# Sums of the latents' squares by one-column matmuls, and the last output block in finer pieces, in a two-layer decoder trunk

## The chip, the core and the metric

The kernel runs on one core of one Trainium2 chip. A core has a matrix engine (TensorE, PE in the profile; PEld is its loading of weights), VectorE (DVE), ScalarE (ACT), GpSimd (POOL) and SyncE (SP, which here only starts transfers). Each engine works through its own list of instructions in order; semaphores make one wait for another. The metric is the device time of one execution in microseconds, as the median of several.

## What is computed

Two layers, one sequence of 1024 tokens, width 1024, all in float32. Cut to what matters here:

```python
for l in range(DEPTH):                                  # 2
    h = x * (1.0 + scale[:, None, :]) + shift[:, None, :]
    (p_cq, p_ckv, p_kr, p_qb, ..., p_gate) = jnp.split(h @ w_in[l], SPLIT_POINTS, axis=-1)
    cq = rms_norm(p_cq, q_norm_g[l])                    # 768 columns
    ckv = rms_norm(p_ckv, kv_norm_g[l])                 # 256 columns
    ...                                                 # three groups of attention heads
    sub = y @ w_out[l]
    x = layer_norm(ALPHA * x + (1.0 + gate[:, None, :]) * sub, ln_g[l], ln_b[l])
```

`rms_norm` divides a token's row by the root of the mean of its squares. The change concerns the sums of squares of `cq` and `ckv`, and the last block of the last layer's `layer_norm`.

## The kernel before

Every float32 matrix is split into a high and a low part, and a product is three matmuls (line 206). Activations are held transposed, features on partitions and tokens in columns. A projection (`project`, line 209) makes 128 features for all tokens, in two halves of 512 columns, each a chain of 24 matmuls into one PSUM bank of the pool `ps_p` (tile `pj`, two banks); a function `evac` then empties the bank. Other banks are `ps_s` (tile `S`, three) for scores, `ps_t` (tile `T`, two) for transposes, and `o_ps` (tile `O`).

Each layer runs the indexer (scores of all keys into `acc`, line 441), then heads B, the selection of 256 keys a row (`select`, 31 rounds of counting over `acc` on VectorE, line 467, and ScalarE, line 485), heads C, heads A, and the output projection. The code names these one after another, but a scheduler interleaves them and fixes each engine's order when the kernel is built; it decides by durations that it assumes, so other instructions can give another order everywhere behind them.

Eight calls of `latent` in each layer make `ckv` (two calls, sums in `rk`) and `cq` (six calls, sums in `scq`). Two of them are called right behind the indexer, before heads B; the others are spread between heads B. For each half, `evac` squares the bank into `sq` (line 614), and the sum over the 128 features, which lie on partitions, is made in two steps: four transposes of 128x128 into a bank `T` (line 619), and a reduction on VectorE of the bank's 512 columns to 4 (line 622 for the first chunk of a sum, line 625 for the later ones, with an addition in line 626). `norm_r` (line 644) then takes the power -1/2 on GpSimd.

The same banks `T` serve the attention's transposes of probabilities (line 320), which ScalarE and VectorE empty (lines 323, 324). GpSimd scales probabilities (line 298), computes low parts of weights (line 198) and multiplies by gates (line 339). Lines 229 to 238 empty the projections of queries and keys; a bank `pj` is free once line 238 has read it.

The output projection (line 853 on) goes over eight blocks of 128 tokens, in each over two halves of 512 columns: 24 matmuls, then on VectorE a product (line 868), an addition (869) and statistics (870); when both halves are done, the statistics are merged, and in the last layer two operations for each half (879, 880) and a store started by SyncE (881) end the block.

Of the kernel before, what the change touches and what calls it, by code (L numbers as in the profile page):

```python
# [8 lines left out]
F32 = mybir.dt.float32  # L9
# [3 lines left out]
AF = mybir.ActivationFunctionType  # L13
OP = mybir.AluOpType
AX = mybir.AxisListType
# [5 lines left out]
S = 1024  # L21
P = 128
# [13 lines left out]
TBO = (7,6,5,4,3,2,1,0)  # L36
# [72 lines left out]
def trunk(ctx: ExitStack, tc: tile.TileContext, a, out):  # L109
# [494 lines left out]
    def latent(l, i):  # L604

        wh, wl = w_chunk(l, CKV + i)
        g = gkv[:, i:i + 1] if i < 2 else gq[:, i - 2:i - 1]
        sums = rk if i < 2 else scq

        def evac(half, cols, ps):  # L610
            hi, lo, sq = RW.next().bitcast(F32R), RW.next().bitcast(F32R), PR.next()
            act.activation(hi, ps, AF.Copy, scale=g)
            dve.scalar_tensor_tensor(lo, ps, g, bc(hi), OP.mult, OP.subtract)
            act.activation(sq, ps, AF.Square)
            for e, part in enumerate((hi, lo)):
                sp.dma_start(cq_d[:, (2 * i + e) * 1024 + half * 512:(2 * i + e) * 1024 + half * 512 + 512], bc(part))
            t = ps_t.tile([P, 4, P], F32, name="T")
            for j in range(4):
                pe.transpose(t[:, j, :], sq[:, j * P:(j + 1) * P], ident)
            to = sums[:, half * 4:half * 4 + 4]  # L620
            if i in (0, 2):
                dve.tensor_reduce(to, t, AX.X, OP.add)
            else:
                s4 = small.tile([P, 4], F32, name="s4")
                dve.tensor_reduce(s4, t, AX.X, OP.add)
                dve.tensor_tensor(to, to, s4, OP.add)

        project(wh, wl, 8, HA, evac)
        if i == 1:
            norm_r(rk, rk, 256, 1e-6, 1.0)  # L630
        elif i == 7:
            norm_r(scq, scq, 768, 1e-6, -float(96 ** -0.5))
# [177 lines left out]
    def out_proj(l):  # L810
        last = l == DEPTH - 1
        order = [3, 4, 5, 6, 7, 0, 1, 2]
        Y = HA
        for k in order[:5]:
            raw = WR.next()
            sp.dma_start(raw, y_d[k])
            act.activation(Y[k][0], raw, AF.Copy)
            (pool if k in YP[l] else dve).tensor_tensor(Y[k][1], raw, bc(Y[k][0]), OP.subtract)  # L818


        Vs = [VS[0][:, i * 1024:(i + 1) * 1024] for i in range(6)]
        f = G.n % 2 ^ 1
        XR = Ring([AC[0], RES] + ([G.tiles[f]] if last else []))
        at = {3: (Vs[4], Vs[5]), 4: (Vs[0], Vs[1]), 5: W.tiles[0:2], 6: W.tiles[2:4],
              7: (fresh(f"g{1 - f}", F32R), fresh("bi1", F32R)), 0: held[0:2], 1: held[2:4],
              2: (Vs[2], [fresh(f"rw{n}", F32R, 512) for n in range(2)])}
        wo = {}
        for k in order:
            raw = WR.next()
            sp.dma_start(raw, a["w_out"][l, k])  # L830
            hi, lo = at[k]
            eng = pool if k in WP[l] else dve
            for n in range(2):
                c = slice(n * 512, n * 512 + 512)
                act.activation(hi[:, c], raw[:, c], AF.Copy)  # L835
                eng.tensor_tensor(lo[n] if k == 2 else lo[:, c], raw[:, c], bc(hi[:, c]), OP.subtract)
            wo[k] = [(hi[:, n * 512:n * 512 + 512], lo[n] if k == 2 else lo[:, n * 512:n * 512 + 512]) for n in range(2)]
        g1 = BI.tiles[0]
        sp.dma_start(g1, g1_d[l].to_broadcast([P, 1024]))
        if last:  # L840
            sp.dma_start(LNG, a["ln_g"][l].to_broadcast([P, 1024]))
            sp.dma_start(LNB, a["ln_b"][l].to_broadcast([P, 1024]))
        else:

            lnc = small.tile([P, 2, 8], F32, name="lnc", bufs=1)
            sp.dma_start(lnc, a["ln_c"])
            dve.tensor_tensor(lnc[:, 0, :], lnc[:, 0, :], scale1_n, OP.mult)
            dve.tensor_tensor(lnc[:, 1, :], lnc[:, 1, :], scale1_n, OP.mult)
            dve.tensor_tensor(lnc[:, 1, :], lnc[:, 1, :], shift_n, OP.add)
        X = Ring(AC[1:4] + [PR3[0]])  # L850
        PR.tiles = [G.tiles[f]]
        xs = {}
        for tb in TBO:
            tok = slice(tb * P, (tb + 1) * P)
            xr = XR.next()
            sp.dma_start(xr, xw_d[tb] if last else a["x"][tb])
            r = X.next()
            st = small.tile([P, 2, 6], F32, name="st")
            for n in range(2):
                cols = slice(n * 512, n * 512 + 512)  # L860
                ps = (ps_p if n else ps_s).tile([P, 512], F32, name="pj" if n else "S")
                items = []
                for k in order:
                    yh, yl = Y[k]
                    w0, w1 = wo[k][n]
                    items += [(yh[:, tok], w0), (yl[:, tok], w0), (yh[:, tok], w1)]
                chain(ps, items)
                dve.tensor_tensor(r[:, cols], ps, g1[:, cols], OP.mult)
                dve.scalar_tensor_tensor(r[:, cols], xr[:, cols], ALPHA, r[:, cols], OP.mult, OP.add)
                dve.bn_stats(st[:, n, :], r[:, cols])  # L870
            mv = small.tile([P, 2], F32, name="mv")
            dve.bn_aggr(mv, st)
            rs = small.tile([P, 1], F32, name="rs")
            dve.tensor_scalar(rs, mv[:, 1:2], 1e-5, None, OP.add)
            pool.tensor_tensor(rs, rs, mhalf, OP.pow)
            if last:
                for n in range(2):
                    cols = slice(n * 512, (n + 1) * 512)
                    dve.scalar_tensor_tensor(r[:, cols], r[:, cols], mv[:, 0:1], LNG[:, cols], OP.subtract, OP.mult)
                    dve.scalar_tensor_tensor(r[:, cols], r[:, cols], rs, LNB[:, cols], OP.mult, OP.add)  # L880
                    sp.dma_start(out[tb][:, cols], r[:, cols])
                continue
            dve.tensor_scalar(r, r, mv[:, 0:1], rs, OP.subtract, OP.mult)
            sp.dma_start(x1_d[tb], r)
            xs[tb] = r
            if len(xs) == 4:
                for k in range(8):
                    t = ps_t.tile([P, 512], F32, name="T")
                    for j in range(4):
                        pe.transpose(t[:, j * P:(j + 1) * P], xs[tb // 4 * 4 + j][:, k * P:(k + 1) * P], ident)  # L890
                    mod_h(t, tb // 4, k, PR.next(), lnc[:, 0, :], lnc[:, 1, :])
                xs = {}
# [193 lines left out]
```

## Time and profile before

| what | us |
|---|---|
| three timed runs | 1753.45, 1750.38, 1753.22 |
| their median | 1753.22 |
| the profiled execution, its own time | 1750.43 |
| its span (first to last instruction) | 1748.6 |

The profile records one execution: for each instruction its engine, source line, start, duration and the idle time of its engine just before it, with the instruction or transfer that ended this idle time. A page sums it up; views of the trace group instructions by line, list who waited for whom, show the order of time in a stretch, or give each engine's busy time in windows. "Granted clock" is the share of TensorE's full clock in a window. The slices of the page below have each 1/40 of the span, and a digit is the busy share in tenths:

```profile
PE   8999899999999999989999999999999899998998
DVE  6888898888588678885772668889876967778777
ACT  4254599895534666675112656999744357667620
```

### The profile page before, as it was taken

What the parts mean: (1) busy time and instruction counts of PE and PEld (TensorE: products, weight loads), DVE (VectorE), ACT (ScalarE), POOL (GpSimd) and SP (SyncE); (2) the same over time, 40 slices, a digit from 0 to 9 for tenths busy, and PEclk for the clock granted to TensorE, in tenths of its full rate; (3) what the DMA queues carried; (4) which work ended last, traced back from release to release, by engine and by line L of the source; (5) the groups of instructions that cost most, each with busy time, mean ns of one, the idle gap of its engine ahead of it and who ended that gap; (6) DMA issues with size and microseconds to landing.
All of it is one profiled execution on the core that took longest, in us unless ns stands there. A gap on an engine that the chain in (4) does not pass through costs nothing.

```text
span 1748.6 us, 26930 instructions
## 1 busy us (share of the span) xinstructions
PE 1673.0 (96%) x9192; PEld 1451.5 (83%) x9192; DVE 1350.5 (77%) x3213; ACT 1019.8 (58%) x2010; POOL 666.9 (38%) x614
## 2 busy tenths in 40 slices
PE   8999899999999999989999999999999899998998
PEld 8888688888887888878898977888789788987886
DVE  6888898888588678885772668889876967778777
ACT  4254599895534666675112656999744357667620
POOL 0221143323434355463346413333243344657421
PEclk9999999999999999999999999999999999999999
DMA  9665023233202521222343421333221227113122
GB/s 367 212 215 189 25 73 97 70 136 91 79 35 54 221 90 58 73 70 93 125 157 124 168 73 49 85 111 95 73 97 50 60 52 265 47 52 124 49 86 95
DMA packets 57668, 187.32 MB, mean 107 GB/s; under 512 B 7862, under 2 KB 8886, under 8 KB 57020
## 3 DMA queue, kind: packets, MB, share of 16 engines
q1 hardware_dynamic: 53116, 156.25, 26.3%
q0 software_dynamic: 4416, 29.36, 5.8%
q8 instruction: 72, 1.18, 0.3%
q14 instruction: 64, 0.52, 0.1%
HBM read 133.94 MB, written 39.07 MB: 99 GB/s over the span
## 4 chain that ended last, share of the span: by engine, by line
PE 53%; DVE 8%; ACT 3%; issue 2%; DMA 1%; POOL 1%; DVEq 0%; ACTq 0%; POOLq 0%
PE pj L204 30%; PE S L204 12%; PE O L332 5%; PE T L320 5%; DVE pt L324 1%; ACT pt L323 1%; PE T L204 1%; ACT scr L485 1%; DVE acc L543 0%; DVE pr L536 0%; DVE acc L441 0%; PE T L890 0%; DVE h L818 0%; DVE acc L291 0%; ACT pr L296 0%
## 5 line engine op out<-in xcount | busy, mean ns | idle before, releaser
L204 PE MATMUL pj<-h,w 128*128 128x512 f32 (+1 forms) x3408 | 833.0, 391 | 13.9 <-DVE qk L238 5.8
L204 PEld LDWEIGHTS pj<-h,w 128*128 128x128 f32 x3408 | 629.9, 190 | 131.1 <-issue 11.9
L198 POOL TENSOR_TENSOR w<-wr,w 128x1024 fp32r<-128x1024 f32 (+2 forms) x86 | 192.4, 2238 | 302.3 <-ACT w L197 290.1
L204 PE MATMUL S<-qk,qk 128*128 128x512 f32 (+2 forms) x1104 | 279.7, 358 | 8.4 <-DVE mx L288 3.1
L323 ACT ACTIVATE pt<-T 128x512 fp32r<-128x512 f32 (+1 forms) x320 | 172.4, 551 | 111.2 <-PE T L320 53.8
L298 POOL TENSOR_SCALAR pr<-pr,den 128x896 f32<-128x896 f32 (+7 forms) x180 | 139.0, 776 | 253.3 <-DVE den L297 223.9
L324 DVE TENSOR_TENSOR pt<-T,pt 128x512 fp32r<-128x512 f32 (+1 forms) x320 | 199.5, 633 | 43.9 <-ACT pt L323 37.9
L332 PE MATMUL O<-pt,v 128*128 128x256 f32 (+1 forms) x1280 | 212.8, 286 | 9.2 <-DVE pt L324 4.1
L485 ACT ACTIVATE scr<-acc,U 128x768 uint8<-128x768 f32 x186 | 193.2, 1038 | 35.6 <-DVE U L481 18.1
L204 PEld LDWEIGHTS S<-qk,qk 128*128 128x128 f32 x1104 | 184.2, 190 | 33.4 <-DVE mx L288 6.4
L332 PEld LDWEIGHTS O<-pt,v 128*128 128x128 f32 x1280 | 186.1, 191 | 26.7 <-DVE pt L324 6.7
L339 POOL TENSOR_TENSOR g<-g,osum 64x256 f32<-64x256 f32 x128 | 98.9, 773 | 235.0 <-DVE osum L337 222.8
L296 ACT ACTIVATE pr<-pr,mx 128x384 f32<-128x384 f32 (+7 forms) x188 | 145.5, 775 | 48.1 <-DVE mx L288 31.2
L320 PE MATMUL T<-ident,pr 128*128 128x128 f32 x852 | 145.4, 279 | 6.3 <-POOL pr L298 3.1
L467 DVE TENSOR_SCALAR_CACHE_REDUCE scr<-acc,U 128x384 uint8<-128x384 f32 x186 | 138.2, 743 | 3.8
L197 ACT ACTIVATE w<-wr 128x1024 fp32r<-128x1024 f32 (+2 forms) x86 | 83.8, 976 | 69.2 <-PE pj L204 59.7
L320 PEld LDWEIGHTS T<-ident,pr 128*128 128x128 f32 x852 | 102.1, 142 | 18.7 <-POOL pr L298 4.2
L204 PE MATMUL pj<-w,h 128*128 128x256 f32 (+2 forms) x672 | 107.0, 300 | 0.2 <-ACT w L835 0.2
L204 PEld LDWEIGHTS pj<-w,h 128*128 128x128 f32 x672 | 91.7, 190 | 5.1 <-ACT w L835 0.5
L336 ACT ACTIVATE osum<-O 64x256 f32<-64x256 f32 x128 | 48.6, 380 | 63.4 <-PE O L332 60.3
L441 DVE SCALAR_TENSOR_TENSOR acc<-S,wi,acc 128x512 f32<-128x512 f32 (+1 forms) x84 | 55.7, 678 | 23.0 <-ACT S L436 22.8
L337 DVE TENSOR_TENSOR osum<-O,osum 64x256 f32<-64x256 f32 x128 | 53.5, 418 | 25.1 <-ACT osum L336 21.4
(282 smaller groups left out, 2512.2 us busy)
## 6 DMA issues: line engine op xcount, KB each, us to landing
wr<-in_wt_dram SPq DMA_DIRECT2D x62, 512.0 KB, 3.9
cq_d<-rw SPq DMA_DIRECT2D x64, 256.0 KB, 2.0
h<-cq_d POOLq DMA_DIRECT2D x4, 4096.0 KB, 19.1
qk<-qk POOLq DMA_DIRECT2D x48, 256.0 KB, 3.0
pt<-in_w_ada_dram SPq DMA_DIRECT2D x22, 512.0 KB, 4.7
wr<-in_w_out_dram SPq DMA_DIRECT2D x16, 512.0 KB, 3.5
bi<-in_bias_dram SPq DMA_DIRECT2D x14, 512.0 KB, 3.7
bi<-in_w_ada_dram SPq DMA_DIRECT2D x10, 512.0 KB, 4.4
```

The lines of the kernel that those rows point to most:

```text
L197: act.activation(hi[:, :n], raw[:, :n], AF.Copy)
L198: (lo_eng or pool).tensor_tensor(lo[:, :n], raw[:, :n], bc(hi[:, :n]), OP.subtract)
L204: pe.matmul(ps, lhsT=l, rhs=r, start=(i == 0), stop=(i == len(items) - 1))
L296: act.activation(p[:, :n], p[:, :n], AF.Exp, bias=m, scale=-1.0, accum_out=den)
L298: (dve if ne[qb] else pool).tensor_scalar(p[:, :n], p[:, :n], den, 0.5, OP.mult, OP.mult)
L320: pe.transpose(t[:, c:c + P], p[j](2 * kp + kk), ident)
L323: act.activation(pt[:, 0, :n], t[:, :n], AF.Copy)
L324: dve.tensor_tensor(pt[:, 1, :n], t[:, :n], bc(pt[:, 0, :n]), OP.subtract)
L332: pe.matmul(o[:, oc], lhsT=vt(kb), rhs=pt[:, e, pc], start=(kb == 0 and e == 0), stop=(kb == 2 * g + 1 and e == 1), skip_group_check=True)
L339: pool.tensor_tensor(yc, yc, s[r0:r0 + 64], OP.mult)
L467: dve.tensor_scalar(scr8[:, :IDX_LEN[b]], scores(b), s, None, op, OP.add, accum_out=dst[:, b:b + 1])
L485: act.activation(scr[:, :IDX_LEN[b]], scores(b), AF.Sign, bias=U[:, b:b + 1].bitcast(F32), accum_out=cnt[:, b:b + 1])
```

## The change

The four transposes of a half become four matmuls with the squares as weights and a column of ones as the moving operand: each gives one column with the sums over the 128 features, for 128 tokens. The 4 columns are copied out by ScalarE, and the additions of later chunks go to GpSimd. Separately, the last block of the last layer makes its second half as two chains of 256 columns, takes its statistics over pieces of 256, and starts its second store from ScalarE's queue.

```diff
-            t = ps_t.tile([P, 4, P], F32, name="T")
+            to = sums[:, half * 4:half * 4 + 4]
+
+            t = ps_t.tile([P, 512], F32, name="T")
             for j in range(4):
-                pe.transpose(t[:, j, :], sq[:, j * P:(j + 1) * P], ident)
-            to = sums[:, half * 4:half * 4 + 4]
+                pe.matmul(t[:, j:j + 1], lhsT=sq[:, j * P:(j + 1) * P], rhs=ones, start=True, stop=True,
+                          skip_group_check=True)
             if i in (0, 2):
-                dve.tensor_reduce(to, t, AX.X, OP.add)
+                act.activation(to, t[:, 0:4], AF.Copy)
             else:
                 s4 = small.tile([P, 4], F32, name="s4")
-                dve.tensor_reduce(s4, t, AX.X, OP.add)
-                dve.tensor_tensor(to, to, s4, OP.add)
+                act.activation(s4, t[:, 0:4], AF.Copy)
+                pool.tensor_tensor(to, to, s4, OP.add)
...
-            st = small.tile([P, 2, 6], F32, name="st")
-            for n in range(2):
-                cols = slice(n * 512, n * 512 + 512)
-                ps = (ps_p if n else ps_s).tile([P, 512], F32, name="pj" if n else "S")
+
+            end = last and tb == TBO[-1]
+            st = small.tile([P, 4, 6], F32, name="st4", bufs=1) if end else small.tile([P, 2, 6], F32, name="st")
+            for o, w in ((0, 512), (512, 256), (768, 256)) if end else ((0, 512), (512, 512)):
+                n, cols = o // 512, slice(o, o + w)
+                bank = (ps_p if n else ps_s).tile([P, 512], F32, name="pj" if n else "S")
+                ps, part = bank[:, :w], slice(o % 512, o % 512 + w)
                 items = []
                 for k in order:
                     yh, yl = Y[k]
                     w0, w1 = wo[k][n]
-                    items += [(yh[:, tok], w0), (yl[:, tok], w0), (yh[:, tok], w1)]
+                    items += [(yh[:, tok], w0[:, part]), (yl[:, tok], w0[:, part]), (yh[:, tok], w1[:, part])]
                 chain(ps, items)
...
-                dve.bn_stats(st[:, n, :], r[:, cols])
+                if end:
+                    for i in range(o, o + w, 256):
+                        dve.bn_stats(st[:, i // 256, :], r[:, i:i + 256])
+                else:
+                    dve.bn_stats(st[:, n, :], r[:, cols])
...
-                    cols = slice(n * 512, (n + 1) * 512)
+                    cols, queue = slice(n * 512, n * 512 + 512), act if end and n else sp
...
-                    sp.dma_start(out[tb][:, cols], r[:, cols])
+                    queue.dma_start(out[tb][:, cols], r[:, cols])
```

What this does to the engines' lists is seen at two places. The first is the junction between the indexer and the selection of layer 0 (layer 1 has the same), VectorE's list with - for before and + for now; `T`, `pj` and `S` are banks, `qk` queries and keys, `rk` the sums of `ckv`, `cnt` counts of the selection:

```order
 L441 SCALAR_TENSOR_TENSOR acc<-S,wi,acc 128x512
-L622 TENSOR_REDUCE rk<-T 128x4
 L467 TENSOR_SCALAR scr,cnt_127<-acc 128x512
 L231 TENSOR_TENSOR qk_76<-pj,qk_76 64x512
 L441 SCALAR_TENSOR_TENSOR acc<-S,wi,acc 128x512
 L446 TENSOR_TENSOR acc<-acc,causb 128x128
-L622 TENSOR_REDUCE rk<-T 128x4
 L238 TENSOR_TENSOR qk_78<-pj,qk_77 64x512
 L467 TENSOR_SCALAR scr,cnt_127<-acc 128x640
-L625 TENSOR_REDUCE s_1551<-T 128x4
+L648 TENSOR_SCALAR rk<-rk 128x8
 L238 TENSOR_TENSOR qk_78<-pj,qk_77 64x512
```

Both reductions ahead of the first line 238 are gone, and the first step of `norm_r` (now line 648) has moved up between the two lines 238. At the same place ScalarE's list now reads:

```order
L229 ACTIVATE qk_76<-pj 64x512
L436 ACTIVATE S<-S 128x512
L624 ACTIVATE rk<-T 128x4 x2
L237 ACTIVATE qk_77<-pj 64x512
L627 ACTIVATE s_1551<-T 128x4
L627 ACTIVATE s_1589<-T 128x4
L237 ACTIVATE qk_77<-pj 64x512
L485 ACTIVATE scr,cnt<-acc,U 128x768
```

The four copies stand between the emptyings of the projection, ahead of the selection's first pass (line 485). The second place is GpSimd's list among the heads B of layer 0, now: `pr` are probabilities, `den` their divisors, `w` parts of weights:

```order
+L628 TENSOR_TENSOR scq<-scq,s_2985 128x4
 L298 TENSOR_SCALAR pr_94<-pr_94,den 128x128
+L628 TENSOR_TENSOR scq<-scq,s_3023 128x4
 L298 TENSOR_SCALAR pr_94<-pr_94,den 128x256
 L198 TENSOR_TENSOR w_87<-wr_92,w_86 128x1024
+L628 TENSOR_TENSOR scq<-scq,s_3064 128x4
 L298 TENSOR_SCALAR pr_95<-pr_95,den 128x384
+L628 TENSOR_TENSOR scq<-scq,s_3102 128x4
 L298 TENSOR_SCALAR pr_95<-pr_95,den 128x512
```

The additions stand between the scalings of probabilities. Behind the junction the scheduler has also put the work of heads B, C and A and of the selection in another order, in both layers; the indexer, and the output projection of the first layer up to the next junction, keep theirs on TensorE.

## The prediction

> **What bounds the kernel now.** First the page: what each engine does and what the chain of waits that ended last is made of.
>
> ```profile
> span 1748.6 us, 26930 instructions
> PE 1673.0 (96%) x9192; PEld 1451.5 (83%) x9192; DVE 1350.5 (77%) x3213; ACT 1019.8 (58%) x2010; POOL 666.9 (38%) x614
> PE 53%; DVE 8%; ACT 3%; issue 2%; DMA 1%; POOL 1%; DVEq 0%; ACTq 0%; POOLq 0%
> ```
>
> TensorE is busy for all but 75.6 us of the span and leads the chain; VectorE comes next with 8%. So work taken from VectorE is worth only what TensorE waits for it. The second view is the list of waits, the third the instructions of the lines that the change touches.
>
> ```profile
> PE T L619 <- DVE rk L622: 7.3, 4, 2.2
> L619 PE MATMUL T<-ident,pr x128: 270/273/477, 192.4 to 1294.2; 128*128 128x128 f32 x128
> L626 DVE TENSOR_TENSOR scq<-scq,s x20: 143/162/1652, 323.9 to 1296.7; 128x4 f32<-128x4 f32 x20
> ```
>
> The first row says (total us, times, longest us): TensorE waited 7.3 us in four waits for the reductions of line 622. They are the stage that matters, once in each layer, where the indexer ends and the selection begins. Third view, the order of time there in layer 0 (start, duration, the idle time and its releaser in brackets), then the two rows that matter in layer 1:
>
> ```profile
> 196.60 1.12 PE L619 MATMUL T<-ident,pr 128*128 128x128 f32 x4 [1.64 <-DVE rk L622]
> 199.50 1.12 PE L619 MATMUL T<-ident,pr 128*128 128x128 f32 x4 [1.79 <-DVE rk L622]
> 200.27 0.78 PE L204 MATMUL pj<-h,w 128*128 128x512 f32 x1
> 195.86 0.68 DVE L622 TENSOR_REDUCE rk<-T 128x4 f32<-128x512 f32 x1
> 196.46 0.68 DVE L467 TENSOR_SCALAR_CACHE_REDUCE scr<-acc 128x512 uint8<-128x512 f32 x1
> 198.76 0.68 DVE L622 TENSOR_REDUCE rk<-T 128x4 f32<-128x512 f32 x1
> 199.48 0.69 DVE L238 TENSOR_TENSOR qk<-pj,qk 64x512 fp32r<-64x512 f32 x1
> 1053.89 0.69 DVE L238 TENSOR_TENSOR qk<-pj,qk 64x512 fp32r<-64x512 f32 x1
> 1054.68 0.78 PE L204 MATMUL pj<-h,w 128*128 128x512 f32 x1
> ```
>
> The third and the fourth group of transposes (196.60, 199.50) wait for a bank T that VectorE must first sum. VectorE itself is hardly idle here. After the last group a long run of projections starts, and its bank is freed at 200.17 by line 238, at the same moment.
>
> The same stretch in windows as long as the clock's steps (columns: length, busy us of PE, PEld, DVE, ACT, POOL with counts, the granted clock, DMA):
>
> ```profile
> 192.87:196.28 3.41, 0.89 (x7) 0.42 (x4) 3.35 (x8) 1.49 (x3) 0.00 (x0) 1.00 0.01 2
> 196.28:199.70 3.42, 1.31 (x5) 0.92 (x6) 3.32 (x8) 0.59 (x1) 0.55 (x1) 0.50 0.00 0
> 199.70:203.11 3.41, 3.41 (x11) 2.83 (x11) 3.25 (x7) 0.00 (x0) 0.33 (x1) 0.50 0.37 77
> 1053.03:1056.44 3.41, 2.52 (x8) 2.22 (x9) 3.28 (x8) 0.00 (x0) 0.57 (x1) 0.50 0.37 77
> 1056.44:1059.85 3.41, 3.41 (x9) 2.64 (x9) 3.35 (x8) 0.00 (x0) 0.51 (x1) 0.50 0.37 77
> 49.51:52.92 3.41, 3.34 (x28) 3.25 (x27) 1.97 (x6) 2.30 (x2) 0.08 (x1) 1.00 0.39 137
> 49.51:52.92 3.41, 1.84 (x16) 1.93 (x16) 1.00 0.39 137
> 52.92:56.33 3.41, 3.41 (x12) 3.41 (x11) 1.93 (x4) 2.30 (x2) 0.00 (x0) 0.50 0.88 282
> ```
>
> After a poorly filled window the clock is granted at 0.50 for two windows, and the first projections run at half speed. The last three rows give a warning: the window at 49.51 is full of TensorE work, but 16 of its 28 matmuls, 1.84 us of it, are the one-column matmuls of line 925 (the row with PE and PEld alone), and the next window gets 0.50. One-column matmuls seem not to hold the clock.
>
> **The change, part by part.**
>
> *TensorE.* 128 transposes become 128 one-column matmuls. Their price is the spacing of the weight loads in a closed run:
>
> ```profile
> 313.57 0.75 PEld L619 LDWEIGHTS T<-ident,pr 128*128 128x128 f32 x7
> 139.91 1.75 PEld L266 LDWEIGHTS O<-ones,g 128*128 128x128 f32 x14
> ```
>
> Transposes: (0.75 - 0.14)/6 = 0.10 us, 0.14 being one load. One-column matmuls with the same ones: (1.75 - 0.19)/13 = 0.12 us, at a load of 0.19. Where TensorE is full the change costs 0.02 us each; the 32 at the junctions below stand in idle time, so 96 x 0.02 = 1.9 us is the upper bound, 0 the lower (single groups differ by as much), and I take **+1.0**.
>
> *VectorE* loses 32 reductions x 0.68 + 24 additions x 0.16 = 25.6 us, of which 8 x 0.68 + 4 x 0.15 = 6.0 stand at the two junctions.
>
> *ScalarE and GpSimd* get 32 copies and 24 additions of 128x4, which no row has. Nearest rows:
>
> ```profile
> L250 ACT ACTIVATE cs<-ccol 128x8 f32<-128x8 f32 x1 | 0.2, 209 | 0.3 <-DMA ccol<-in_c_dram 0.3
> L336 ACT ACTIVATE osum<-O 64x256 f32<-64x256 f32 x128 | 48.6, 380 | 63.4 <-PE O L332 60.3 <-POOL pr L298 0.7
> L1076 POOL MEMSET const-float32-1.0<- 128x1 f32 x1 | 0.1, 98 | 0.0
> L339 POOL TENSOR_TENSOR g<-g,osum 64x256 f32<-64x256 f32 x128 | 98.9, 773 | 235.0 <-DVE osum L337 222.8 <-PE pj L204 7.0 <-PE T L320 3.9
> ```
>
> A copy costs 0.21 (near the 8-column row) to 0.38 us; an addition 0.10 to 0.77, and I take 0.2, twice the one-column fill. That is 6.7 and 4.8 us on engines 58% and 38% busy, hidden by their idle time; where the cover fails is the slower rival below.
>
> *The junctions.* ScalarE is almost idle there (1.49 and 0.59 us in the first two windows), so the banks come free early and all four groups are done near 196. TensorE then waits for the projection bank, that is for line 238. Ahead of it VectorE loses both reductions of line 622: 196.46 - 195.86 = 0.60 and 199.48 - 198.76 = 0.72, together 1.32 us. The projections start at 198.95 in place of 200.27; only 1.3 of the 5 us idle are won, since line 238 is late next. The wait that is added, VectorE's line 648 for two additions on GpSimd, has the second line 238 and the selection queued behind it; but the additions can end near 198, and VectorE arrives near 199.7, so it costs nothing unless an addition takes over 0.77.
>
> Those 1.32 us lie at half clock: worth 0.66 if both half-speed windows stay. In layer 1 the window from 1053.03 would now be filled but for 0.3 us, and if that ends the half speed at 1056.44, the work done by 1059.85 is 3.08/2 + 3.41 = 4.95 in place of 5.17/2 = 2.59: worth 2.4. How the windows fall differs between executions, so I take the middle, 1.5 a junction, **-3.1** (bounds -1.3 to -4.8).
>
> *The rest of the selection.* 25.6 - 6.0 = 19.6 us leave VectorE in these stretches:
>
> ```profile
> 210.00:560.00 350.00, 340.41 (x1862) 291.37 (x1861) 287.58 (x769) 248.32 (x484) 127.49 (x119) 1.00 0.26 79
> 1060.00:1300.00 240.00, 236.85 (x1224) 200.49 (x1223) 204.53 (x602) 198.54 (x385) 83.06 (x80) 0.99 0.28 87
> ```
>
> TensorE idles only 9.6 + 3.2 = 12.8 us in them. VectorE loses 4% of its 492 us; 4% of the idle time is **-0.5**, bounds 0 and -12.8. The scheduler also puts the work of both stretches in another order; the rows cannot price that, and it adds a few us either way to the range.
>
> *The last block.* The chain for columns 512 to 1023 becomes two of 256 columns, so that VectorE's last three operations are half as long.
>
> ```profile
> 1734.71 5.45 PE pj L204 x24
> 1358.36 3.12 PE L204 MATMUL pj<-w,h 128*128 128x256 f32 x24
> 1741.64 0.69 DVE L870 BATCH_NORM_STATS2 st<-pr 128x6 f32<-128x512 f32 x1
> L441 DVE SCALAR_TENSOR_TENSOR acc<-S,wi,acc 128x512 f32<-128x512 f32 x27 | 20.0, 748 | 17.5 <-ACT S L436 17.4
> L441 DVE SCALAR_TENSOR_TENSOR acc<-S,wi,acc 128x256 f32<-128x256 f32 x7 | 3.3, 476 | 0.7 <-ACT S L436 0.7
> 1744.00 1.41 DVE L880 SCALAR_TENSOR_TENSOR pr<-pr,rs,lnb 128x512 f32<-128x512 f32 x2
> 1744.78 0.99 SPq L881 DMA_DIRECT2D out_dram<-pr  x2
> ```
>
> TensorE pays: (3.12 - 0.28)/23 = 0.1235 us for each of 48 is 5.93 against 5.45, +0.5. VectorE gains 748 - 476 = 0.27 on each of three operations, -0.8; for the statistics (0.69 at 512) no row at 256 exists, and their part lies between 0 and 0.27. The second store on ScalarE's queue gains nothing: SyncE's two issues end at 1745.77, 0.36 after the data at 1745.41, so the second never stood behind the first. Net **-0.3** (-0.6 to 0).
>
> Sum: +1.0 - 3.1 - 0.5 - 0.3 = **-2.9 us**. The profiled execution took 1750.43 in all (span 1748.6) and would take 1747.5; the three timed runs have the median 1753.22, and would give 1750.3. I forecast the middle, 1751.8 - 2.9 = **1748.9**.
>
> **The rivals.** B, *the half speed goes*. For it: the waits of TensorE get shorter. Against it: the four groups of one column would leave the window at 192.87 as empty for the clock as the one at 49.51. If it went in both layers, the junctions give 1.32 + 2.84/2 = 2.7 and 1.32 + 5.17/2 = 3.9, 6.6 in place of 3.1, and the time is 1748.9 - 3.5 = 1745.4. The Trainium skill (TensorE: Matmul & The Clock Gate, section on what's actually happening) has the clock fall after at least one idle window of some 3.4 us, which by itself would spare a 2.9 us gap like the new one. The trace disagrees: no window above was idle, and 0.89 of 3.41 busy was too little.
>
> C, *the junctions give nothing*: what TensorE wins it loses at its next wait for the same VectorE, and neither they nor the stretches give anything: 1751.8 + 1.0 - 0.3 = 1752.5. For it: 96% busy, so a start 1.3 us earlier may meet the next late operand; against it: VectorE itself runs 3 us ahead after the junction.
>
> D, *slower*: copies stand behind selection passes on ScalarE, additions behind copies on GpSimd, and GpSimd's scaling of line 298 behind additions.
>
> ```profile
> L485 ACT ACTIVATE scr<-acc,U x186: 920/1041/1161, 207.5 to 1255.0; 128x768 uint8<-128x768 f32 x62, 128x896 uint8<-128x896 f32 x62, 128x1024 uint8<-128x1024 f32 x62
> POOL pr L298 <- DVE den L297: 223.9, 113, 9.0
> ```
>
> Line 298 stands directly behind an addition in 9 places, and a copy can wait for one pass, 1.04 us and 0.19 for its accumulator. If all 9 delay TensorE it costs 11.1: 1748.9 + 11.1 = 1760.0; with half of them the time is 1754.5, a loss of 2.7. It decides where an addition ends later than the reciprocal that line 298 has always waited for; those waits (113, 2 us each) speak for slack.
>
> **How the numbers follow.** Forecast 0.50 (own range 1744.5 to 1751), B 0.11, C 0.21, D 0.18. About 0.2%, 3.5 us, can be told from no change. Faster (under 1748.3): 0.35 of the forecast, which a larger gain in the stretches or at the junctions would bring, and B, together 0.46. Same (to 1755.3): the rest of the forecast, 0.16 of C and 0.05 of D, 0.36. Slower: 0.05 of C and 0.13 of D, 0.18. The range takes in B, the larger gains and most of D: 1741 to 1758.
>
> **What would show it.** Right: no wait of TensorE for line 622's successors, projections at 198.9 released by line 238, selection some 3 us earlier, copies near 0.2 us, the last VectorE chain 0.8 shorter after a TensorE chain 0.5 longer. Wrong: clock 1.00 after the junctions (B), waits of line 298 for line 628 or of line 628 for ScalarE (D), or idle time of TensorE that moves by over 5 us in the attention stretches, which would be the new order rather than the operations.

## The result, and the profile after

| | us |
|---|---|
| before, four runs | 1750.38 to 1753.45, median 1752.40 |
| the change, four runs | 1769.47 to 1773.03, median 1770.32 |
| ratio, with its 95% interval | 1.0107 [1.0095, 1.0120] |
| span of the profiled execution | 1769.3 (before 1748.6) |

The change makes the kernel slower by 18 us, past the upper end of the range (1758). The page of the changed kernel has the answer in its second line:

```profile
span 1769.3 us, 27269 instructions
PE 1696.0 (96%) x9344; PEld 1474.3 (83%) x9344; DVE 1329.2 (75%) x3161; ACT 1021.5 (58%) x2042; POOL 672.7 (38%) x638
PE 68%; DVE 17%; ACT 8%; issue 4%; DMA 2%; POOL 1%; SPq 0%; DVEq 0%; ACTq 0%; POOLq 0%
```

TensorE's idle time (span less busy) is 73.3 us against 75.6 before: no engine has begun to hold it up. Its busy time has grown by 23.0 us, and its instructions by 152. Of these the last block has 24. The other 128 stand in the groups of the line of the sums (count, busy us, mean ns of one, idle time before them and what ended it); the first row is the kernel before:

```profile
L619 PE MATMUL T<-ident,pr 128*128 128x128 f32 x128 | 20.7, 291 | 9.7 <-DVE rk L622 7.3 <-DVE acc L441 2.4
L621 PEld LDWEIGHTS T<-ones,pr 128*128 128x128 f32 x256 | 35.0, 213 | 2.7 <-ACT rk L624 1.0 <-DVE acc L441 0.9
L621 PE MATMUL T<-ones,pr 128*128 128x1 f32 x256 | 34.5, 261 | 0.8 <-ACT rk L624 0.8
```

The code asks for 128 one-column matmuls; the record has 256 weight loads and 256 matmuls. A matmul of plain float32 operands is two such pairs here, a transpose of the same 128x128 block was one. (The matmuls of the projections are recorded once each, 24 rows for a chain of 24: the kernel marks their operands as `float32r`, and the views print `f32` for both.) In the order of time, 16 loads for the eight matmuls of two halves take 1.98 us:

```profile
324.56 1.98 PEld L621 LDWEIGHTS T<-ones,pr 128*128 128x128 f32 x16
```

At the junction of layer 0 TensorE's order of time is now:

```profile
194.47 1.05 PE L621 MATMUL T<-ones,pr 128*128 128x1 f32 x8
195.93 4.54 PE L621 MATMUL T<-ones,pr 128*128 128x1 f32 x24 [0.41 <-ACT rk L624]
201.04 5.49 PE L204 MATMUL pj<-h,w 128*128 128x512 f32 x12 [0.58 <-DVE qk L238]
```

The waits for line 622 (7.3 us at both junctions) are gone; 0.41 us is left here, 0.8 at both. In the kernel before, the first group of transposes there began at 192.44 and the projections at 200.27, 7.83 us later; now it is 201.04 - 194.47 = 6.57. In windows of the clock's steps (length, busy us of PE, PEld, DVE, ACT, POOL with counts, granted clock, DMA):

```profile
193.37:196.78 3.41, 3.00 (x20) 2.12 (x18) 3.38 (x9) 2.51 (x7) 0.00 (x0) 1.00 0.01 2
196.78:200.19 3.41, 3.41 (x18) 3.41 (x18) 3.31 (x8) 0.94 (x3) 0.20 (x1) 0.50 0.00 0
200.19:203.61 3.42, 2.84 (x8) 2.28 (x8) 3.30 (x8) 0.77 (x2) 2.19 (x3) 0.50 0.30 61
203.61:207.02 3.41, 3.41 (x9) 2.64 (x9) 3.20 (x11) 0.05 (x1) 0.76 (x2) 0.50 0.47 97
```

The first two windows are 88% and 100% busy, mostly with one-column matmuls, and still three steps are granted at half clock, one more than before. In layer 1 three steps follow too.

Away from the junctions no drop of the clock begins behind the sums. The next two rows (TensorE alone) are a window with 16 one-column matmuls, 1.70 us of it, and its successor; the last two are a window without any, but with gaps, and its successor:

```profile
323.07:326.48 3.41, 3.41 (x25) 1.00 0.38 154
326.48:329.89 3.41, 3.41 (x20) 1.00 0.00 0
282.11:285.53 3.42, 1.73 (x9) 1.00 0.24 84
285.53:288.94 3.41, 3.06 (x15) 0.50 0.24 84
```

Ahead of the last block the trace has 19 steps at half clock, where the kernel before had 14. Six of the 19 stand at the two junctions, where four stood. The drops elsewhere begin behind windows in which line 621 does not run, as at 282.11 (TensorE busy for 1.73 of 3.42 us).

### The profile page after: what moved, and what is told of

Its sections match the earlier page's. It is cut to its first block, busy times and chain, and to the rows that moved or that the text cites. A ratio compares the mean times of both kernels' runs of the same rounds, so it can differ in the third digit from the quotient of the medians.

```text
span 1769.3 us, 27269 instructions
## 1 busy us (share of the span) xinstructions
PE 1696.0 (96%) x9344; PEld 1474.3 (83%) x9344; DVE 1329.2 (75%) x3161; ACT 1021.5 (58%) x2042; POOL 672.7 (38%) x638
## 4 chain that ended last, share of the span: by engine, by line
PE 68%; DVE 17%; ACT 8%; issue 4%; DMA 2%; POOL 1%; SPq 0%; DVEq 0%; ACTq 0%; POOLq 0%
PE pj L204 40%; PE S L204 13%; PE O L332 6%; PE T L320 5%; ACT scr L485 3%; DVE pt L324 2%; ACT pt L323 1%; DVE scr L467 1%; DVE pr L288 1%; DVE pr L536 1%; ACT pr L296 1%; PE T L204 1%; DVE g L261 1%; DVE acc L441 1%; PE S L920 1%
## 5 line engine op out<-in xcount | busy, mean ns | idle before, releaser
L204 PE MATMUL S<-qk,qk 128*128 128x384 f32 (+2 forms) x1104 | 279.0, 359 | 7.5 <-DVE mx L288 4.7
L288 DVE CUSTOM_DVE_ANT_0 pr<-S,bi 128x384 f32<-128x384 f32 (+2 forms) x96 | 52.3, 554 | 32.3 <-PE T L320 26.8
```

The source lines that it names most:

```text
L204: pe.matmul(ps, lhsT=l, rhs=r, start=(i == 0), stop=(i == len(items) - 1))
```

## Three theories, and a sum to test

**Price**: 256 load-and-matmul pairs in place of 128, on an engine that is full. **Clock**: one-column matmuls do not hold the granted clock. **Queues** (rival D of the prediction): ScalarE's copies and GpSimd's additions come late, and line 298 behind them.

The first two can be added up from each trace. At full clock neighbouring starts lie apart by a mean 0.106 us for the one-column matmuls (198 pairs of the changed kernel) and 0.111 us for transposes (213 pairs of the run that doubles them): 27.2 us against 14.2, +13.0. A step of 3.41 us at half clock does up to 1.7 us less work. With 19 of them for 14 that is up to +8.5. (This counts the steps of the profiled execution, whatever took the clock down.) With 0.5 for the last block's finer chain, TensorE's busy time should be 1673.0 + 13.0 + 8.5 + 0.5 = 1695.0; it is 1696.0. The same sum, each with its own spacing and steps, for the runs below:

| kernel | median us | ratio to before | TensorE busy us | by the sum | idle us | half-clock steps |
|---|---|---|---|---|---|---|
| before | 1752.40 | | 1673.0 | | 75.6 | 14 |
| the change | 1770.32 | 1.0107 [1.0095, 1.0120] | 1696.0 | 1695.0 | 73.3 | 19 |
| sums only | 1768.94 | 1.0102 [1.0084, 1.0119] | 1696.6 | 1696.2 | 74.1 | 20 |
| last block only | 1751.50 | 0.9994 [0.9982, 1.0006] | 1676.5 | 1678.6 | 72.8 | 17 |
| transposes twice | 1764.89 | 1.0083 [1.0064, 1.0101] | 1686.5 | 1688.9 | 75.7 | 15 |
| one column, twice | 1817.18 | 1.0376 [1.0361, 1.0391] | 1743.6 | 1742.0 | 72.1 | 30 |
| 128 equal columns | 1758.76 | 1.0039 [1.0026, 1.0052] | 1687.2 | 1687.2 | 73.7 | 13 |
| bfloat16 squares | 1746.83 | 0.9968 [0.9955, 0.9982] | 1662.9 | 1662.8 | 82.1 | 14 |
| copies on VectorE | 1774.12 | 1.0134 [1.0103, 1.0166] | 1692.1 | 1690.0 | 77.4 | 16 |

The sum holds within 2.4 us in all of them, and the idle time of the float32 kernels stays between 72 and 78 us. Most edits also give another built order; with the sums left out, about two thirds of TensorE's list in the change stand as before. The idle time shows that the new order does not make TensorE wait longer in total; whether it moved some half-clock steps is not separated.

## The experiments

**Which part.** The change's sums with the last block of before, and the other way round (each is the change with one part of the first diff undone).

> The last output block is as before; only the sums of squares are changed. Three theories of the 18 us by which the change is slower. Price: each one-column float32 matmul of the code is recorded as two weight loads and two matmuls 0.116 us apart, so 128 of them cost 256 x 0.116 = 29.7 us on a TensorE that is full, where the 128 transposes cost 128 x 0.104 = 13.3 us, +16 us. Clock: matmuls of one column do not hold the granted clock; 5 more windows of 3.4 us at half speed, up to 8.5 us. Queues: ScalarE's copies and GpSimd's additions come late, and the selection's scaling at line 298 behind them. All three lie in the sums, so all three expect about the time of the change, 1768 to 1773 us. Only if the last block's finer pieces cost the time would this be near 1752 us.

> Only the last output block is changed, with the sums by transposes as before. Price, clock and queues: about the time before, 1750 to 1754 us (24 more matmul instructions and one shorter last chain on VectorE, between -1.3 and +0.5 us). If the last block were the cause: near 1770 us.

Measured: 1768.94 and 1751.50 us. The whole loss lies in the sums; the last block is within its interval of no change.

**What 128 instructions are worth.**

```diff
             for j in range(4):
-                pe.transpose(t[:, j, :], sq[:, j * P:(j + 1) * P], ident)
+                for _ in range(2):
+                    pe.transpose(t[:, j, :], sq[:, j * P:(j + 1) * P], ident)
```

> The kernel before, with each of the 128 transposes of the squares made twice into the same place: 128 TensorE instructions more, all else as before; the output is the same. Price: instructions on a full TensorE reach the time one for one, so +128 x 0.104 = +13.3 us, 1763 to 1767 us, with no more half-speed windows than before (14). Clock: transposes hold the clock, and what 128 instructions cost is small beside it, so 1752 to 1757 us. Queues: no copy or addition is moved, 1752 to 1757 us.

Measured: 13.6 us more than the kernel before (1764.89 against 1751.32 of the same chip). 128 instructions on TensorE reach the time nearly one for one (128 x 0.111 = 14.2), with one half-clock step more and the same idle time; price expected this, clock and queues did not.

**One-column matmuls twice.**

```diff
-            for j in range(4):
+            for j in (0, 0, 1, 1, 2, 2, 3, 3):
                 pe.matmul(t[:, j:j + 1], lhsT=sq[:, j * P:(j + 1) * P], rhs=ones, start=True, stop=True,
```

> The changed kernel, with each one-column matmul made twice into the same column: 128 more in the code, 256 more in the record if each is two; the output is the same. Price: +256 x 0.116 = +29.7 us, 1797 to 1803 us. Clock: the longer runs of one-column matmuls take the clock down in more windows, beyond the price: over 1803 us, with over 24 windows at half speed (19 with the change). Queues: copies and additions are as many as in the change, so 1770 to 1776 us.

Measured: 1817.18 us, 47 above the change, and 30 half-clock steps. The price that was expected (29.7) misses by 17, the 11 further steps (up to 18.7) fill it. Where the clock falls is plain among the heads B of layer 0, in the order of time and in windows of TensorE alone:

```profile
326.36 1.09 PE L204 MATMUL pj<-h,w 128*128 128x512 f32 x4
327.28 0.46 PE L332 MATMUL O<-pt,v 128*128 128x256 f32 x3
327.57 4.55 PE L621 MATMUL T<-ones,pr 128*128 128x1 f32 x32
331.99 0.77 PE L204 MATMUL S<-qk,qk 128*128 128x256 f32 x2
```

```profile
326.75:330.16 3.41, 3.41 (x30) 1.00 0.02 5
330.16:333.58 3.42, 3.42 (x15) 0.50 0.30 123
333.58:336.99 3.41, 3.41 (x10) 0.50 0.08 30
336.99:340.41 3.42, 3.42 (x28) 1.00 0.01 2
```

The window at 326.75 has no idle time at all; from 327.57 on, over two thirds of it, it holds one-column matmuls, and the next two steps are at 0.50. Behind seven windows without idle time come 14 of the 30 steps in this trace, one to four each. In six of them the one-column matmuls take over 2.5 us, and no window with that much of them kept the clock. In the seventh, at 1081.10, they take 1.69 us, while other full windows with 1.7 to 1.9 us of them kept it, as the change's own at 323.07 does; so where the line lies is not settled.

**128 equal columns.** The same matmuls and loads, with the column of ones read 128 times:

```diff
-                pe.matmul(t[:, j:j + 1], lhsT=sq[:, j * P:(j + 1) * P], rhs=ones, start=True, stop=True,
+                pe.matmul(t[:, j * P:(j + 1) * P], lhsT=sq[:, j * P:(j + 1) * P], rhs=ones.to_broadcast([P, P]), start=True, stop=True,
                           skip_group_check=True)
             if i in (0, 2):
-                act.activation(to, t[:, 0:4], AF.Copy)
+                act.activation(to, t[:, 0:512:P], AF.Copy)
             else:
...
```

> The changed kernel, with the column of ones read 128 times, so that each of its matmuls has 128 moving columns instead of one, and every 128th column copied: as many matmuls and weight loads, the same sums. Price and clock together (+16 us for the instructions, up to 8.5 us for the extra half-speed windows, less the wait at line 622 that the change takes away): the instructions stay at about 0.116 us apart, but 128 columns hold the clock as the transposes did, so the half-speed windows go back from 19 to 14 to 16 and the time to 1760 to 1766 us. Price alone: what the columns are makes no difference to the clock, 1768 to 1773 us. Queues: copies and additions are those of the change, 1768 to 1773 us. If an instruction of 128 float32 columns takes longer than one of a single column, the time is later by 256 times the difference, which the row of the line shows.

Measured: 1758.76 us, 11.6 less than the change, a little below the 1760 to 1766 us of price and clock together, though its matmuls do 128 times the arithmetic. Their group has the same count, and they stand 0.116 us apart instead of 0.106:

```profile
L621 PE MATMUL T<-ones,pr 128*128 128x128 f32 x256 | 33.3, 277 | 0.6 <-ACT rk L624 0.6
```

The half-clock steps fall from 19 to 13. At the junction (windows of this kernel):

```profile
197.50:200.92 3.42, 3.11 (x26) 2.83 (x24) 3.32 (x8) 1.39 (x5) 0.20 (x1) 1.00 0.00 0
200.92:204.33 3.41, 1.38 (x7) 1.04 (x6) 3.28 (x8) 0.77 (x2) 0.98 (x3) 1.00 0.29 60
204.33:207.74 3.41, 3.41 (x9) 2.65 (x9) 3.31 (x7) 0.00 (x0) 1.97 (x2) 0.50 0.39 80
207.74:211.16 3.42, 3.42 (x16) 2.81 (x15) 1.81 (x9) 0.66 (x2) 0.00 (x0) 1.00 0.09 18
```

A window that is 91% busy with 128-column matmuls is followed by full clock; one step at half clock is left where three were. Together with the windows of the run before, full of one-column matmuls and followed by 0.50, this shows for the junctions that the columns count, and not only the engine's being occupied. The steps elsewhere also fell, and for those no cause is shown. The Trainium skill (TensorE: Matmul & The Clock Gate, section on what's actually happening) lets the clock fall after an idle window. These runs show a window without idle time after which it falls.

**One pair instead of two.** Squares and ones in bfloat16. This kernel leaves out the low bits of the squares, so its output is another, and only its time is of use:

```diff
-            hi, lo, sq = RW.next().bitcast(F32R), RW.next().bitcast(F32R), PR.next()
+            hi, lo, sq = RW.next().bitcast(F32R), RW.next().bitcast(F32R), PR.next().bitcast(BF16)[:, 0:512]
...
-                pe.matmul(t[:, j:j + 1], lhsT=sq[:, j * P:(j + 1) * P], rhs=ones, start=True, stop=True,
+                pe.matmul(t[:, j:j + 1], lhsT=sq[:, j * P:(j + 1) * P], rhs=ones_b, start=True, stop=True,
```

> The changed kernel, with the squares and the column of ones in bfloat16: the squares are rounded before they are summed. Price: a matmul is then one weight load and one matmul in the record, 128 instead of 256, each at most 0.116 us after the one before, so at least 14.8 us less than the change: 1748 to 1756 us. Clock: the one-column matmuls take at most half the time, so of the 5 extra half-speed windows between none and all go; as the only cause it would give 1762 to 1770 us. Queues: copies and additions are as in the change, 1768 to 1773 us.

Measured: 1746.83 us, below the lower end.

```profile
L623 PE MATMUL T<-ones_b,pr 128*128 128x1 bf16 x128 | 7.1, 166 | 3.0 <-ACT rk L626 3.0
```

```profile
322.73 0.26 PEld L623 LDWEIGHTS <-pr 128*128 128x128 bf16 x8 [0.15 <-issue]
```

The group of the line has 128 in the record, and the order of time shows eight loads in 0.26 us: by the starts they stand 0.028 us apart, much closer than assumed. TensorE's busy time falls by 10.1 us against before, but the time by only 6: the idle time has grown by 6.5. The list of waits (total us, times, longest) tells where, first of this kernel, then of the kernel before:

```profile
PE pj L206 <- DVE qk L240: 16.5, 8, 4.4
```

```profile
PE pj L204 <- DVE qk L238: 5.8, 6, 2.6
```

Line 240 here is line 238 before, VectorE's emptying of queries and keys. The Trainium skill (FP8 and Floating Point Precision, section on TensorE precision) counts four passes for true float32. The record here shows two pairs for it, and one for bfloat16.

**Copies on VectorE.**

```diff
-                act.activation(to, t[:, 0:4], AF.Copy)
+                dve.tensor_copy(to, t[:, 0:4])
             else:
-                s4 = small.tile([P, 4], F32, name="s4")
-                act.activation(s4, t[:, 0:4], AF.Copy)
-                pool.tensor_tensor(to, to, s4, OP.add)
+                dve.tensor_tensor(to, to, t[:, 0:4], OP.add)
```

> The changed kernel, but VectorE copies the four sums out of the bank (or adds them to the running sums straight from it), so no ScalarE copy and no GpSimd addition; the one-column matmuls stay. Price and clock: the same 256 instructions and about the same half-speed windows, and at the end of each indexer the wait for VectorE's sums comes back (7.3 us before line 619 in the kernel before, 0.8 us with the change), so 1770 to 1778 us. Queues: ScalarE and GpSimd lose 32 copies and 24 additions, and the time goes back toward 1752 us, below 1762 us.

Measured: 1774.12 us, as price and clock expected. Without a single copy on ScalarE or addition on GpSimd nothing is won back, so the queues are not the cause, though the wait for VectorE's sums that comes back (4.3 us in this trace) could hide a small gain. In the change itself their rows read:

```profile
L627 ACT ACTIVATE s<-T 128x4 f32<-128x4 f32 x24 | 3.9, 165 | 9.9 <-PE T L621 9.8
L628 POOL TENSOR_TENSOR scq<-scq,s 128x4 f32<-128x4 f32 x20 | 3.9, 198 | 33.5 <-ACT s L627 33.4
```

GpSimd does wait for ScalarE's copies, 33.4 us in all, the sign that the prediction named for D. But TensorE's idle time has not grown with it.

**Fewer sums: adding first.** If TensorE's instructions set the time, 96 transposes less should be worth 10 us. GpSimd adds the squares of a norm's slices, and only the total is transposed and summed:

```diff
+            part = slice(half * 512, half * 512 + 512)
             if i in (0, 2):
+                pool.tensor_copy(RES[:, part], sq)
             else:
+                pool.tensor_tensor(RES[:, part], RES[:, part], sq, OP.add)
+            if i in (1, 7):
+                t = ps_t.tile([P, 4, P], F32, name="T")
+                for j in range(4):
+                    pe.transpose(t[:, j, :], RES[:, half * 512 + j * P:half * 512 + (j + 1) * P], ident)
+                dve.tensor_reduce(sums[:, half * 4:half * 4 + 4], t, AX.X, OP.add)
```

> Another way to the same sums, from the kernel before: GpSimd adds the squares of the slices of a norm element by element into one buffer, and only the total is transposed and summed, so 32 transposes instead of 128, and 8 sums on VectorE instead of 32. The last block is as before. Price: -96 x 0.104 = -10.0 us, and up to 7.3 us less waiting for VectorE's sums, against two additions of 512 columns at the end of a norm (1.3 us each by the row of line 730): 1738 to 1745 us. Clock: the transposes that go held the clock no worse than what follows them, so windows at half speed stay at 14 or fewer. Queues: 32 more passes of about 1.3 us on GpSimd put 42 us in front of the selection's scaling at line 298, which gives 1752 to 1765 us if that is on the path.

Then the same with the additions on VectorE (the first slice squared straight into the buffer), and with the total summed by 128 equal columns and a copy on ScalarE:

> As adding first on GpSimd, but the squares of a norm are added on VectorE (24 additions of 512 columns, 0.687 us each by the rows of that size) and the first slice of a norm is squared by ScalarE straight into the buffer: 32 transposes instead of 128, VectorE's own work 24 x 0.455 = 11 us smaller than before less the longer first steps, GpSimd as before. The run before it gave back its 10.7 us of TensorE time in waits. If GpSimd's passes of 1.29 us caused those waits: 1738 to 1744 us. If VectorE is the bound in the stretches where TensorE arrives early (97% busy between 1360 and 1400 us already in the kernel before), the gain is given back again, TensorE's idle time grows to 80 us or more from 75.6, and the time is 1745 to 1753 us.

> As the last, but the total of a norm is summed by matmuls with 128 equal columns of ones and copied by ScalarE: 32 in the code, 64 in the record, 64 x 0.116 = 7.4 us on TensorE against 32 x 0.111 = 3.6 us, and 8 sums of 0.69 us less on VectorE. If VectorE is the bound where TensorE arrives early, taking these sums away at the end of each indexer is worth their 5.5 us less up to 3.9 us: between 3 us faster and 2 us slower than the kernel with transposes of the total, 1743 to 1753 us. If TensorE alone set the time: 2 to 4 us slower than it, 1742 to 1748 us.

| kernel | median us | ratio to before | TensorE busy us | idle us | half-clock steps |
|---|---|---|---|---|---|
| added on GpSimd | 1756.32 | 1.0017 [1.0005, 1.0029] | 1668.1 | 87.6 | 19 |
| added on VectorE | 1773.66 | 1.0150 [1.0123, 1.0177] | 1669.4 | 100.7 | 24 |
| added on VectorE, 128 columns | 1775.16 | 1.0138 [1.0117, 1.0160] | 1674.3 | 101.4 | 23 |

The first misses what price expected and lies in the range of queues (1752 to 1765); the other two miss every range, by over 20 us. Whether GpSimd's passes cost the first its gain stays open, since the second takes them away but puts the additions on VectorE. Its forecast went by 11 us less work there; VectorE is busy 1361.9 us, 11.4 more than before. The sums themselves take some 8 us less, and other operations, as many as before, take longer; why is open. TensorE has less to do in the first two and waits longer in all three. Two windows show where, the first of the kernel before, the second of adding on GpSimd; then two rows from the list of waits of adding on VectorE:

```profile
1360.00:1400.00 40.00, 35.54 (x185) 29.89 (x184) 38.74 (x52) 11.99 (x21) 15.42 (x10) 0.96 0.23 66
```

```profile
1360.00:1400.00 40.00, 29.84 (x135) 24.34 (x134) 39.23 (x38) 8.92 (x15) 25.59 (x12) 0.85 0.41 134
```

```profile
PE pj L204 <- DVE qk L238: 26.6, 8, 8.8
PE pj L204 <- DVE v L364: 8.6, 1, 8.6
```

In this stretch VectorE is full in both kernels (38.74 and 39.23 of 40 us), and TensorE stands still for 10 us of it instead of 4.5. In the version with additions on VectorE the waits for lines 238 and 364 alone are 35 us, against 8 before. So in the stretch shown what TensorE saves is given back where VectorE is full, and more half-clock steps (19 to 24) add to it; why one version has 25 us more idle time than before and another 12 is not settled. The built order of VectorE's list differs among these kernels, and its part was not separated from that of VectorE's load.

**Two bfloat16 parts.** Each square is split into two bfloat16 parts, both summed into the same column, so that only the last bits are lost:

```diff
             act.activation(sq, ps, AF.Square)
+            act.activation(s0, sq, AF.Copy)
+            pool.tensor_tensor(s1, sq, s0, OP.subtract)
...
-                pe.matmul(t[:, j:j + 1], lhsT=sq[:, j * P:(j + 1) * P], rhs=ones, start=True, stop=True,
-                          skip_group_check=True)
+                for n, s in enumerate((s0, s1)):
+                    pe.matmul(t[:, j:j + 1], lhsT=s[:, j * P:(j + 1) * P], rhs=ones_b, start=n == 0, stop=n == 1,
+                              skip_group_check=True)
```

> The changed kernel, with each square split into two bfloat16 parts (ScalarE copies the first, GpSimd subtracts it, 512 columns each) and both summed into the same column by one-column bfloat16 matmuls: 256 in the record, but 0.028 us apart by the trace of the run with rounded squares, so 7.1 us on TensorE against 14.2 us for the transposes and 27 us for the change. Price and clock: 3.5 us above the run with rounded squares (1746.8 us), half-speed windows at 14 to 16, so 1747 to 1754 us, if ScalarE's 32 copies and GpSimd's 32 subtractions (1.29 us each by the row of its additions) lie beside other work. If these are on the path at the end of each indexer (two halves a layer wait for about 1.7 us more): up to 7 us more, 1754 to 1761 us.

Measured: 1773.05 us (1.0117 [1.0100, 1.0134]), a miss. TensorE is busy 1680.1 us and idle 90.2, with 23 half-clock steps: the price came out (0.028 us apart), but neither the idle time nor the clock did (14 to 16 steps were expected). What made them is open.

**Only where TensorE waits.** At the junctions TensorE waits for VectorE in any case, so there the second pair should cost nothing and the relief of VectorE should count. The kernel before, with 128 equal columns, ScalarE and GpSimd for the first two slices of a layer alone:

```diff
             for j in range(4):
-                pe.transpose(t[:, j, :], sq[:, j * P:(j + 1) * P], ident)
+                if i < 2:
+                    pe.matmul(t[:, j, :], lhsT=sq[:, j * P:(j + 1) * P], rhs=ones.to_broadcast([P, P]),
+                              start=True, stop=True, skip_group_check=True)
+                else:
+                    pe.transpose(t[:, j, :], sq[:, j * P:(j + 1) * P], ident)
...
+            if i == 0:
+                act.activation(to, t[:, :, 0], AF.Copy)
+            elif i == 1:
+                s4 = small.tile([P, 4], F32, name="s4")
+                act.activation(s4, t[:, :, 0], AF.Copy)
+                pool.tensor_tensor(to, to, s4, OP.add)
```

> The kernel before, with the sums made by matmuls (128 equal columns of ones), ScalarE's copies and GpSimd's additions for the first two slices alone, those at the end of each indexer; the other six slices of a layer keep transposes and VectorE, and the last block is as before. There TensorE waits for VectorE: from the first of these instructions to the projections pass 7.83 us before, 6.57 us with the change and 6.59 us with 128 columns, so the price of 64 instructions lies in a wait. Price and clock: 1.25 us gained at each of the two places, one half-speed window less at each (1.7 us), nothing lost elsewhere: 1745 to 1751 us. If the order that follows from it costs what it cost where squares were added first (TensorE idle 88 to 101 us against 75.6 us): 1755 to 1772 us.

Measured: 1747.82 us against 1751.08, ratio 0.9981 [0.9971, 0.9992]: 0.2% faster than the kernel before, as expected. Its page, and its order of time at the junction of layer 0:

```profile
span 1744.7 us, 26980 instructions
PE 1671.9 (96%) x9224; PEld 1451.9 (83%) x9224; DVE 1343.0 (77%) x3201; ACT 1021.2 (59%) x2018; POOL 667.3 (38%) x618
```

```profile
192.23 1.16 PE L620 MATMUL T<-ones,pr 128*128 128x128 f32 x8
193.70 3.09 PE L620 MATMUL T<-ones,pr 128*128 128x128 f32 x24 [0.31 <-ACT rk L626]
198.82 7.55 PE L204 MATMUL pj<-h,w 128*128 128x512 f32 x25 [2.03 <-DVE qk L238]
```

From the first sum to the projections pass 6.59 us, 1.24 less than before, the 64 pairs lie in the wait, and 10 half-clock steps are left of 14. In layer 1 it is 6.58 us (1044.42 to 1051.00). Two of the four steps that are gone stood at the junctions. TensorE's idle time is 72.8 us, so nothing is given back. The built order is here nearly that of the kernel before (about 98% of TensorE's list, against 68 to 84% in the other runs with changed sums); that may be part of why it came out as worked out.

## Why the prediction was wrong

- **TensorE's price** is the step that failed: "128 transposes become 128 one-column matmuls", at 0.02 us each, +1.0. The spacing of 0.12 us in the row of line 266 was read rightly (0.119 in the run of 16 above), but it is the spacing of the record's pairs, and there are 256 of them. That row already showed it: it has 14 loads in one run, where a call of `part_sums` makes eight matmuls. The term is +13.0. What the transposes cost (0.10 expected, 0.111 measured) was nearly right.
- **The clock** was seen and not priced. The prediction said "One-column matmuls seem not to hold the clock", and then let the junctions keep or lose the half speed that they had. The trace shows five steps more, up to 8.5 us, but only two of them, up to 3.4 us, behind windows with the new matmuls; the cause of the other three is open. The profiled execution was also the one with the lowest granted clock: by the mean of all four executions (0.982, against 0.984 of the kernel before in the experiments) the loss is nearer 4 us. With 128 columns TensorE's busy time falls by 8.8 us, although their spacing costs some 2.5 us more.
- **The junctions** gave the time that was worked out, in part by luck: 1.32 us expected at each, 1.26 measured in layer 0 and 1.24 in layer 1 (7.82 us in the first fence below, of the kernel before; 6.58 in the second). But the four groups were to be done near 196, 3.6 us after the start of the first, with TensorE idle until line 238. They take 6.0 us, twice as many pairs and about half of them at half clock, and end 0.58 us ahead of the projections; in layer 1 no wait for line 238 is left. So the price is paid here too, and only a wait that had room for it hid it. The value put on them, 3.1, did not come: the half speed there lasts a step longer instead of shorter.

```profile
1046.86 0.66 PE L619 MATMUL T<-ident,pr 128*128 128x128 f32 x4
1054.68 13.58 PE L204 MATMUL pj<-h,w 128*128 128x512 f32 x48
```

```profile
1051.75 1.05 PE L621 MATMUL T<-ones,pr 128*128 128x1 f32 x8
1058.33 13.73 PE L204 MATMUL pj<-h,w 128*128 128x512 f32 x48
```

- **VectorE's relief** (21.3 us less busy, 25.6 expected) is worth the 2.3 us by which TensorE's idle time falls, junctions and stretches together, less than the 3.1 and 0.5 put down for them.
- **ScalarE and GpSimd**: 0.165 and 0.198 us measured, 0.21 and 0.2 expected. D, the slower rival, had the direction of the result by another cause.
- **The last block**: from the start of the chain for columns 512 on to the end of VectorE's work 10.86 us before (1734.55 to 1745.41), 10.43 now (the first row is the kernel before):

```profile
1734.55 1.52 PE L204 MATMUL pj<-v,h 128*128 128x512 f32 x6
1755.68 0.88 PE L204 MATMUL pj<-v,h 128*128 128x256 f32 x6
1764.70 1.41 DVE L889 SCALAR_TENSOR_TENSOR pr<-pr,rs,lnb 128x512 f32<-128x512 f32 x2
```

That is -0.43 where -0.3 was expected.

The sum that would have been right for the profiled execution: +13.0 + 8.5 + 0.5 on TensorE, -2.3 idle, 19.7 of the 20.7 us by which its span grew. With 4 us for the clock, as in the mean of the executions, it is 15.2 of the 18 us between the medians, and some 3 us stay open. The price is the larger part either way, and the part that the experiments show.

## What to carry to other kernels

Price a new instruction by its count in the record, not in the code: compare a nearby line's count with the loops that made it, above all for float32 matmuls. A matmul with few columns can cost twice, by its weight load and, in long runs, by the clock of what follows; where it must be, try to give it columns to read or put it where the engine waits anyway. And work taken from the leading engine is worth something only where no other engine is full in the same stretch.

## What the hardware showed

- Two load-and-matmul pairs in the record for one matmul of plain float32 (256 for 128), one for a float32 transpose (128 for 128) and for a bfloat16 matmul (128 for 128).
- Their spacing with 128x128 weights, at full clock: 0.106 us with one float32 column, 0.116 with 128 columns, 0.111 for a transpose, 0.028 with one bfloat16 column. A float32 matmul of 128 columns thus costs hardly more than one of a single column.
- With one-column matmuls made twice, the granted clock fell to 0.50 for one to four steps behind each of six windows of 3.41 us in which TensorE was never idle and one-column matmuls took over 2.5 us. With the change, full windows with 1.7 to 1.9 us of them kept it.
